# Hybrid decoder block on one core: the first modulation and the first norm made in another way

## The chip, the cores and the metric

The kernel runs on one core of a Trainium2 chip. The metric is the device time of one execution in microseconds (us): the median of three runs of the kernel before is 2028.79 (2028.37 to 2030.98). PE is TensorE (products), PEld its weight loads, DVE is VectorE, ACT is ScalarE, POOL is GpSimd, SP is SyncE, which here only issues loads.

## The reference

One sequence of 256 tokens with 2048 channels passes a decoder block. What matters here is its first step: a vector `c` gives a modulation, and the input's first norm is scaled and shifted by it before it meets the weights `w_in`.

```
c_act = silu(c)
mod = c_act @ w_ada + b_ada            # 2048 x 12288; sh1, sc1, g1, sh2, sc2, g2
h = rms_norm(x, norm1_g) * (1 + sc1) + sh1
x = x + g1 * hybrid_mixer(h, ...)      # h @ w_in, attention and SSD branches
h = rms_norm(x, norm2_g) * (1 + sc2) + sh2
x = x + g2 * swiglu(h, ...)
return rms_norm(x, final_g)
```

The norm divides each token by the root of the mean of its squares over the 2048 channels. `sh1` and `sc1` need the first 4096 columns of `w_ada`.

## The kernel before, in words

Everything is kept with channels on the 128 partitions and the 256 tokens along the free axis, so x is 16 tiles (`xs0`, `KT` = 16). Weights come from HBM in entries of one megabyte (128 x 2048), one load each, in a fixed list (`entries`); SP issues them (line 135) as buffers come free. Each weight entry is split by `Job.split`: ACT copies it to a rounded high part `wh` (line 181), DVE takes the difference as low part `wl` (line 182). Products are three matmuls per tile: high by high, high by low and low by high (lines 727 to 729).

The first products, with the first 5120 columns of `w_in` (`add_parts`), need h. Since h needs the modulation, and that needs 32 MB of `w_ada`, the 16 channel tiles are taken in five parts (`PARTS` = 2, 3, 4, 4, 3): once the modulation of a part's tiles is there, PE runs through all 40 output tiles with those tiles alone, and adds to partial sums. Sums of the first eight output tiles stay in PSUM (`res`); those of the others cycle through three banks (`cyc`) and are evacuated to SBUF (`part`) by ACT (line 696) or DVE.

The modulation of a part is made on DVE (`ada1_entries`): each row block of `w_ada` is multiplied by its element of `c_act` and added to an accumulator `aacc` (lines 403, 405), and at the end PE sums `aacc` over the partitions with single-column matmuls (`finish`, line 415: `aacc` is the weight, a column of ones the moving operand). DVE adds biases and gains (417 to 419), scales x (424), and ACT and DVE write h in a high and a low half (425, 426). The first part has four entries, loaded before everything else but x, which is loaded ahead of the fourth.

The first norm (`norm1`) is made once: ACT squares each of the 16 tiles (375), PE multiplies it by a matrix of ones and adds all up (376), so each partition has each token's sum; `inv_rms` takes the root on ACT (315) and the reciprocal on DVE (316), over 256 columns. Until x is there PE runs 14 products of ones (`warm`, line 383), whose result nothing uses.

The order of the instructions on each engine is fixed when the program is built; an engine works its list in that order, and each instruction waits for what it needs.

Of the kernel before, what the change touches and what calls it, by code (L numbers as in the profile page):

```python
# [9 lines left out]
F32 = mybir.dt.float32  # L10
F32R = mybir.dt.float32r
AF = mybir.ActivationFunctionType
ALU = mybir.AluOpType
# [3 lines left out]
P = 128  # L17
NACC = 4
NRES = 8
ZLEAD = 9  # L20
NWARM = 14
NCYC = 3
AHEAD = 2
BG = (4, 8, 8, 24, 4)
# [3 lines left out]
PARTS = (2, 3, 4, 4, 3)  # L28
NS = 40
L = 256  # L30
D = 2048
KT = D // P
# [3 lines left out]
LEAD1 = 2048 // (2048 // (256 * PARTS[0]) * 128)  # L36
# [11 lines left out]
def hybrid_block_kernel(  # L48
# [24 lines left out]
    act, dve, pool, pe = nc.scalar, nc.vector, nc.gpsimd, nc.tensor  # L73
# [12 lines left out]
    tmp = open_pool(ctx, "tmp", 2)  # L86
# [5 lines left out]
    cyc = [pcy.tile([P, 2, L], F32, name=f"cyc{i}") for i in range(NCYC)]  # L92
# [17 lines left out]
    def ps_side(name):  # L110
        return banks["side"].tile([P, 512], F32, tag="ps", name=name)
# [3 lines left out]
    state = {"loaded": 0, "done": 0}  # L115
# [68 lines left out]
    jobs = []  # L184
# [96 lines left out]
    ident = cst.tile([P, P], F32, name="ident")  # L281
    make_identity(nc, ident)
    ones = cst.tile([P, P], F32, name="ones")
# [17 lines left out]
    dve.tensor_scalar(cact, cc[:, C_C : C_C + 16], 0.5, None, op0=ALU.mult)  # L301
    dve.scalar_tensor_tensor(cact, ctmp, 1.0, cact, op0=ALU.add, op1=ALU.mult)
    dve.tensor_scalar(cc[:, C_CW : C_CB + 48], cc[:, C_CW : C_CB + 48], 0.5, None, op0=ALU.mult)

    d_z = dr.tile([32, P, L], F32, name="d_z")
    d_sa = dr.tile([16, P, L], F32, name="d_sa")
# [7 lines left out]
    def inv_rms(dst, ps, n):  # L314
        act.activation(dst, ps, AF.Sqrt, bias=eps[: dst.shape[0]], scale=1.0 / n)
        dve.reciprocal(dst, dst)
# [45 lines left out]
    p0 = open_pool(st0, "p0")  # L362
# [3 lines left out]
    def load_x():  # L366
        for q in range(4):
            nc.sync.dma_start(xs0[:, 4 * q : 4 * q + 4], x[4 * q : 4 * q + 4].rearrange("k p t -> p k t"))

    def norm1():  # L370

        ps = ps_side("n1")[:, :L]
        for k in range(KT):
            sq = tmp.tile([P, L], F32, tag="zv" if k % 2 else "zt", name="sq")
            act.activation(sq, xs0[:, k], AF.Square)
            pe.matmul(ps, ones, sq, start=(k == 0), stop=(k == KT - 1))
        inv_rms(xr, ps, D)

    def warm():

# [4 lines left out]
    def ada1_entries(k0, n):  # L385

        w = 256 * n
        per = 2048 // w
        off = 16 * P * 256 * k0
        res = []  # L390

        def fn_for(a, b):
            def fn(raw):
                if a == 0:
                    state["acc"] = p0.tile([P, 256 * max(PARTS)], F32, tag="aacc", name=f"aacc{k0}", bufs=2)
                acc = state["acc"][:, :w]
                hw = w // 2 if b == KT else w
                for c in range(0, w, hw):
                    for k in range(a, b):
                        o = w * (k - a) + c  # L400
                        r, v = raw[:, o : o + hw], acc[:, c : c + hw]
                        if k == 0:
                            dve.tensor_scalar(v, r, cact[:, 0:1], None, op0=ALU.mult)
                        else:
                            dve.scalar_tensor_tensor(v, r, cact[:, k : k + 1], v, op0=ALU.mult, op1=ALU.add)
                if b == KT:
                    with tc.high_priority(400):
                        finish(acc)

            return fn  # L410

        def finish(acc):
            ps = ps_side(f"ada{k0}")
            for b in range(2 * n):
                pe.matmul(ps[:, b : b + 1], acc[:, b * P : b * P + P], ones[:, 0:1], start=True, stop=True)
            sl = slice(k0, k0 + n)
            dve.tensor_tensor(s1[:, sl], ps[:, 0:n], cc[:, C_BADA + k0 : C_BADA + k0 + n], op=ALU.add)
            dve.tensor_tensor(a1[:, sl], ps[:, n : 2 * n], cc[:, C_BADA + 16 + k0 : C_BADA + 16 + k0 + n], op=ALU.add)
            dve.scalar_tensor_tensor(
                a1[:, sl], a1[:, sl], 1.0, cc[:, C_N1 + k0 : C_N1 + k0 + n], op0=ALU.add, op1=ALU.mult  # L420
            )
            for k in range(k0, k0 + n):
                x_, a_, s_ = xs0[:, k], a1[:, k : k + 1], s1[:, k : k + 1]
                dve.scalar_tensor_tensor(x_, x_, a_, xr, op0=ALU.mult, op1=ALU.mult)
                act.activation(h[:, k, :L], x_, AF.Identity, bias=s_)
                dve.scalar_tensor_tensor(h[:, k, L:], x_, s_, h[:, k, :L].bitcast(F32), op0=ALU.add, op1=ALU.subtract)
            if k0 + n == KT:
                st0.close()
                open_a1()

        for a in range(0, KT, per):
            b = min(a + per, KT)
            src = ada1[off + P * w * a : off + P * w * b].rearrange("(p f) -> p f", p=P)
            res.append((src, fn_for(a, b)))
        return res
# [273 lines left out]
    def add_parts():  # L709

        flat, k0 = [], 0
        starts, adas = [], []
        for r, n in enumerate(PARTS):
            starts.append(len(flat))
            adas.append(ada1_entries(k0, n))
            flat += [(r, m, k, k - k0, n) for m in range(NS) for k in range(k0, k0 + n)]
            k0 += n
        starts.append(len(flat))

        def body(tiles):  # L720
            def fn(wh, wl):
                for t, (r, m, k, c, n) in enumerate(tiles):
                    bank = res[m // 2] if m < NRES else cyc_at(r * NPAIR + (m - NRES) // 2)[2]
                    acc = bank[:, m % 2]

                    first = c == 0 and m % 2 == 0 and (r == 0 if m < NRES else r not in SEEDED)
                    pe.matmul(acc, wh[:, t], h[:, k, :L], start=first, stop=False, skip_group_check=True)  # L727
                    pe.matmul(acc, wh[:, t], h[:, k, L:], start=False, stop=False, skip_group_check=True)  # L728
                    pe.matmul(acc, wl[:, t], h[:, k, :L], start=False, stop=(c == n - 1), skip_group_check=True)  # L729
                    if c == n - 1 and m % 2:  # L730
                        part_done(r, m - 1)

            return fn

        entries.extend(adas[0])
        for g in range(len(flat) // 16):
            jobs.append(Job(w_s[g], body(flat[16 * g : 16 * g + 16])))
            for r in range(NP_ - 1):
                a, b = (max(0, (starts[i] - 16) // 16) for i in (r, r + 1))
                if a <= g < b:  # L740
                    q = adas[r + 1]
                    entries.extend(q[len(q) * (g - a) // (b - a) : len(q) * (g - a + 1) // (b - a)])
        state["nx"] = len(entries)
        state["nl"] = jobs[starts[NP_ - 1] // 16 - 1].entry
# [532 lines left out]
    hook(jobs[NS + 2], lambda: (flush(), gens.append(index_gen())))  # L1277
    hook(jobs[first_pair], open_a2)
    warm()
    load_to(LEAD1 - 1)  # L1280
    load_x()
    load_to(LEAD1)
    norm1()
    run_jobs()
    flush()
    drain()
# [119 lines left out]
```

## Time and profile before

| | |
|---|---|
| median of 3 runs | 2028.79 us |
| the profiled execution | 2029.8 us |
| its span | 2028.1 us |
| DVE busy | 1460.4 us (72%) |
| ACT busy | 1057.4 us (52%) |
| mean DMA rate over the span | 243 GB/s |

The span runs from the first to the last instruction of the program; the execution's own time has some 1.7 us around it. A matmul of f32 operands shows up as two passes in the trace; so the 14 warm-up products are 28 rows. Two passes overlap, so a group's mean is longer than the distance from one to the next. The granted clock is a share of 2.4 GHz: 0.50 is 1.2 GHz.

### The profile page before, as it was taken

Reading aid. Unit: us, or ns where it says so; the run is one execution under the profiler, and the core shown is the slowest. Engines: PE = TensorE matmul, PEld = TensorE weight load, DVE = VectorE, ACT = ScalarE, POOL = GpSimd, SP = SyncE. Lnnn points to the kernel's source line nnn. Section 1 sums busy time; section 2 is a strip of 40 time slices with the busy share of each in tenths; the row PEclk is TensorE's granted clock in tenths of the full one; section 3 lists DMA queues with packets and bytes.
Section 4 is the critical chain, followed back from the end, with each engine's and each line's share of the span. In section 5 each row is a group of like instructions: output and inputs, shape, how many; then the busy total and the mean of one; then the engine's idle time right before and its main releaser. Section 6 shows DMA issues by size and latency. Waiting matters only on the chain.

```text
span 2028.1 us, 31920 instructions
## 1 busy us (share of the span) xinstructions
PE 1988.5 (98%) x12964; PEld 1791.2 (88%) x12964; DVE 1460.4 (72%) x1832; ACT 1057.4 (52%) x1427; POOL 159.5 (8%) x161
## 2 busy tenths in 40 slices
PE   8999999999999999999999999999999999999997
PEld 6899998899888888898989988888888888888887
DVE  6777787977678898888888865668786555544443
ACT  4655475565345766677654444554444444443442
POOL 0000000220000111101113211000000000000000
PEclk8999999999999999999999999999999999999999
DMA  9888767666887767666676876467776555565552
GB/s 376 333 304 303 271 230 276 223 243 235 296 325 257 254 230 261 245 230 246 220 263 231 284 263 218 163 227 274 282 275 218 192 192 187 192 224 189 193 183 100
DMA packets 102339, 492.30 MB, mean 243 GB/s; under 512 B 10768, under 2 KB 45952, under 8 KB 48688
## 3 DMA queue, kind: packets, MB, share of 16 engines
q1 hardware_dynamic: 100528, 486.19, 66.8%
q0 software_dynamic: 704, 3.15, 0.4%
q8 instruction: 102, 1.67, 0.3%
q10 hardware_dynamic: 960, 0.92, 0.1%
q14 instruction: 45, 0.37, 0.1%
HBM read 475.44 MB, written 17.92 MB: 243 GB/s over the span
## 4 chain that ended last, share of the span: by engine, by line
PE 77%; issue 8%; DVE 7%; DMA 4%; ACT 3%; POOL 0%; SPq 0%; DVEq 0%; ACTq 0%; POOLq 0%
PE acc_gu L250 15%; PE acc_gu L252 8%; PE acc_dn L250 7%; PE acc_cv L250 6%; PE acc_dn L252 4%; PE acc_cv L252 4%; DVE wl L182 3%; PE acc_z L250 3%; PE acc_out L250 2%; PE acc_pb L210 2%; PE cyc L729 2%; PE cyc L727 2%; PE acc_pb L211 2%; PE acc_pb L212 2%; PE cyc L728 2%
## 5 line engine op out<-in xcount | busy, mean ns | idle before, releaser
L182 DVE TENSOR_TENSOR wl<-raw,wh 128x2048 fp32r<-128x2048 f32 (+1 forms) x316 | 722.1, 2286 | 319.0 <-ACT wh L181 311.5
L181 ACT ACTIVATE wh<-raw 128x2048 fp32r<-128x2048 f32 (+1 forms) x316 | 599.2, 1897 | 390.8 <-PE acc_dn L250 95.1
L250 PE MATMUL acc_gu<-h,wh 128*128 128x512 f32 x1312 | 313.1, 391 | 0.0
L250 PEld LDWEIGHTS acc_gu<-h,wh 128*128 128x128 f32 x1312 | 241.1, 188 | 46.7
L250 PE MATMUL acc_cv<-h,wh 128*128 128x512 f32 x768 | 193.7, 402 | 0.0
L252 PEld LDWEIGHTS acc_gu<-h,wl 128*128 128x128 f32 x1312 | 168.2, 191 | 6.4
L449 DVE SCALAR_TENSOR_TENSOR acc<-raw,cact,acc 128x1024 f32<-128x1024 f32 x120 | 156.7, 1306 | 23.4 <-DMA raw<-in_ada_dram 22.9
L250 PEld LDWEIGHTS acc_cv<-h,wh 128*128 128x128 f32 x768 | 142.2, 191 | 32.7 <-issue 4.6
L252 PE MATMUL acc_gu<-h,wl 128*128 128x256 f32 x1312 | 170.2, 283 | 0.0
L250 PE MATMUL acc_dn<-ffact,wh 128*128 128x512 f32 x660 | 160.0, 392 | 0.0
L727 PE MATMUL cyc<-h,wh 128*128 128x256 f32 x512 | 148.0, 290 | 5.1 <-ACT cyc L702 1.8
L729 PE MATMUL cyc<-h,wl 128*128 128x256 f32 x512 | 144.9, 288 | 2.9 <-DVE wl L182 2.9
L728 PE MATMUL cyc<-h,wh 128*128 128x256 f32 x512 | 146.3, 286 | 0.0
L210 PE MATMUL acc_pb<-y,wh 128*128 128x256 f32 x512 | 145.6, 284 | 0.0
L211 PE MATMUL acc_pb<-y,wh 128*128 128x256 f32 x512 | 143.1, 279 | 0.0
L212 PE MATMUL acc_pb<-y,wl 128*128 128x256 f32 x512 | 142.8, 279 | 0.0
L250 PEld LDWEIGHTS acc_dn<-ffact,wh 128*128 128x128 f32 x660 | 120.2, 188 | 23.1
L250 PE MATMUL acc_z<-h,wh 128*128 128x512 f32 x512 | 123.1, 393 | 0.0
L250 PEld LDWEIGHTS acc_z<-h,wh 128*128 128x128 f32 x512 | 93.9, 188 | 20.6 <-issue 2.3
L727 PEld LDWEIGHTS cyc<-h,wh 128*128 128x128 f32 x512 | 99.9, 195 | 7.8 <-ACT cyc L702 3.0
L252 PEld LDWEIGHTS acc_cv<-h,wl 128*128 128x128 f32 x768 | 99.0, 191 | 5.0 <-issue 1.2
L252 PE MATMUL acc_cv<-h,wl 128*128 128x256 f32 x768 | 102.4, 284 | 0.0
(331 smaller groups left out, 3357.7 us busy)
## 6 DMA issues: line engine op xcount, KB each, us to landing
raw<-in_w_gu_dram SPq DMA_DIRECT2D x88, 1024.0 KB, 4.7
raw<-in_ada_dram SPq DMA_DIRECT2D x75, 1024.0 KB, 5.1
raw<-in_w_ssm_dram SPq DMA_DIRECT2D x48, 1024.0 KB, 5.2
raw<-in_w_dn_dram SPq DMA_DIRECT2D x44, 1024.0 KB, 4.7
raw<-in_w_z_dram SPq DMA_DIRECT2D x32, 1024.0 KB, 5.1
raw<-in_w_pb_dram SPq DMA_DIRECT2D x32, 1024.0 KB, 5.1
raw<-in_w_s_dram SPq DMA_DIRECT2D x27, 1024.0 KB, 6.3
raw<-in_w_pa_dram SPq DMA_DIRECT2D x16, 1024.0 KB, 5.9
```

The source lines that it names most:

```text
L181: act.activation(whf[:, o], raw[:, o], AF.Copy)
L182: dve.tensor_tensor(wlf[:, o], raw[:, o], whf[:, o].bitcast(F32), op=ALU.subtract)
L210: pe.matmul(acc, wh, rhs[:, :L], start=first, stop=False)
L211: pe.matmul(acc, wh, rhs[:, L:], start=False, stop=False)
L212: pe.matmul(acc, wl, rhs[:, :L], start=False, stop=last)
L250: pe.matmul(acc, wh[:, t], rhs(k), start=n == 0, stop=False, skip_group_check=True)
L252: pe.matmul(acc[:, :L], wl[:, t], rhs(k)[:, :L], start=False, stop=n == end, skip_group_check=True)
L449: dve.scalar_tensor_tensor(a, r, cact[:, k : k + 1], a, op0=ALU.mult, op1=ALU.add)
L727: pe.matmul(acc, wh[:, t], h[:, k, :L], start=first, stop=False, skip_group_check=True)
L728: pe.matmul(acc, wh[:, t], h[:, k, L:], start=False, stop=False, skip_group_check=True)
L729: pe.matmul(acc, wl[:, t], h[:, k, :L], start=False, stop=(c == n - 1), skip_group_check=True)
```

## The change

The first part's modulation is no longer accumulated on DVE. As each of its four entries lands, PE takes every 128 x 128 block of it as weight and the column `cact[:, k]` as moving operand, and adds over the 16 row blocks in PSUM: 64 matmuls of one column (new line 418). The other four parts stay as they were. The squares of x are taken two tiles at a time on ACT and added by DVE to one tile of 512 columns; PE sums that over the partitions into two columns of 128 tokens (new line 386), root and reciprocal are taken of these two columns, and two matmuls with the identity spread the result over all partitions into a PSUM bank (394), from which DVE scales x; a copy goes to `xr` for the later parts. The table for the root is loaded near the start (304). x is loaded after all four entries, the warm-up has 6 products in place of 14, `aacc` has one buffer in place of two, and the first weight entry is split in four pieces of 512 columns. `finish` is cut into `finish`, `modulation` and `scale`.

```
-NWARM = 14
+NWARM = 6
...
+    act.activation(ctmp[:, 0:1], eps, AF.Sqrt)
...
+    def squares():
+        for k in range(0, KT, 2):
+            sq = p0.tile([P, 2, L], F32, tag="sq", name="sq", bufs=2) if k else state["sum"]
+            act.activation(sq, xs0[:, k : k + 2], AF.Square)
+            if k:
+                dve.tensor_tensor(state["sum"], state["sum"], sq, op=ALU.add)
...
     def norm1():
-        ps = ps_side("n1")[:, :L]
-        for k in range(KT):
-            sq = tmp.tile([P, L], F32, tag="zv" if k % 2 else "zt", name="sq")
-            act.activation(sq, xs0[:, k], AF.Square)
-            pe.matmul(ps, ones, sq, start=(k == 0), stop=(k == KT - 1))
-        inv_rms(xr, ps, D)
+        ps = cyc[1][:, 0]
+        for i in range(2):
+            for c in range(2):
+                pe.matmul(
+                    ps[:, c : c + 1], state["sum"][:, i, c * P : c * P + P], ones[:, 0:1],
...
+        r = tmp.tile([P, 2], F32, tag="rcol", name="rcol")
+        inv_rms(r, ps[:, 0:2], D)
+        n1["r"] = cyc[2][:, 0]
+        for c in range(2):
+            pe.matmul(n1["r"][:, c * P : c * P + P], r[:, c : c + 1].to_broadcast([P, P]), ident, start=True, stop=True)
...
             def fn(raw):
+                if k0 == 0:
+                    if a == 0:
+                        state["ps"] = ps_side("ada0")
+                    for k in range(a, b):
+                        for i in range(2 * n):
+                            o = w * (k - a) + i * P
+                            pe.matmul(
+                                state["ps"][:, i : i + 1], raw[:, o : o + P], cact[:, k : k + 1],
...
+                    if b == KT:
+                        with tc.high_priority(400):
+                            squares()
+                            norm1()
+                            for v in (s1, a1):
+                                dve.tensor_copy(v[:, 0:2], state["sum"][:, :, 0])
+                            modulation(state["ps"])
+                            scale(n1["r"])
+                            act.activation(xr, n1["r"], AF.Copy)
+                    return
...
-            jobs.append(Job(w_s[g], body(flat[16 * g : 16 * g + 16])))
+            jobs.append(Job(w_s[g], body(flat[16 * g : 16 * g + 16]), piece=512 if g == 0 else 2048))
...
     warm()
-    load_to(LEAD1 - 1)
+    load_to(LEAD1)
     load_x()
-    load_to(LEAD1)
-    norm1()
+    state["sum"] = p0.tile([P, 2, L], F32, name="sum")
     run_jobs()
```

What the change does to the lists. PE at the start of the program, before (`cyc` is the warm-up's bank, `n` the norm's sums, `ada` the modulation, `res` the first products):

```order
L383 MATMUL cyc_70<-ones 128x512 x14
L376 MATMUL n_174<-sq,ones 128x256 x16
L415 MATMUL ada_254<-ones,aacc_231 128x1 x4
L727 MATMUL res_76<-h,wh_270 128x256
L727 MATMUL res_77<-h,wh_270 128x256
```

And PE at the same place in the changed kernel (`part` is where the entries of `w_ada` land, `sum` the sum of squares, `rcol` the root's two columns):

```order
L400 MATMUL cyc_70<-ones 128x512 x6
L418 MATMUL ada_174<-cact,part 128x1 x64
L386 MATMUL cyc_71<-ones,sum 128x1 x4
L394 MATMUL cyc_72<-ident,rcol 128x128 x2
L772 MATMUL res_76<-h,wh_286 128x256
```

The 64 single-column matmuls now stand ahead of the norm's, and both ahead of the first product.

DVE from the first accumulation on, before (`aacc_231` is the first part's accumulator, `aacc_275` the second part's):

```order
L403 TENSOR_SCALAR aacc_231<-part,cact 128x512
L405 SCALAR_TENSOR_TENSOR aacc_231<-part,cact,aacc_231 128x512 x11
L405 SCALAR_TENSOR_TENSOR aacc_231<-part,cact,aacc_231 128x256 x5
L316 RECIPROCAL xr<-xr 128x256
L405 SCALAR_TENSOR_TENSOR aacc_231<-part,cact,aacc_231 128x256 x3
L182 TENSOR_TENSOR wl_271<-part,wh_270 128x2048
L417 TENSOR_TENSOR s_110<-ada_254,cc 128x2
L418 TENSOR_TENSOR a_109<-ada_254,cc 128x2
L403 TENSOR_SCALAR aacc_275<-rawy,cact 128x768
L419 SCALAR_TENSOR_TENSOR a_109<-a_109,cc 128x2
L405 SCALAR_TENSOR_TENSOR aacc_275<-rawy,cact,aacc_275 128x768
L424 SCALAR_TENSOR_TENSOR xs_148<-xs_148,a_109,xr 128x256 x2
```

DVE at the same place in the changed kernel (the second part's accumulator is now `aacc_297`):

```order
L379 TENSOR_TENSOR sum<-sum,sq 128x512 x7
L428 COPY s_110<-sum 128x2
L428 COPY a_109<-sum 128x2
L460 TENSOR_TENSOR s_110<-ada_174,cc 128x2
L461 TENSOR_TENSOR a_109<-ada_174,cc 128x2
L317 RECIPROCAL rcol<-rcol 128x2
L462 SCALAR_TENSOR_TENSOR a_109<-a_109,cc 128x2
L469 SCALAR_TENSOR_TENSOR xs_149<-xs_149,a_109,cyc_72 128x256 x2
L182 TENSOR_TENSOR wl_287<-part,wh_286 128x512
L471 SCALAR_TENSOR_TENSOR h<-xs_149,s_110,h 128x256 x2
L182 TENSOR_TENSOR wl_287<-part,wh_286 128x512 x3
L442 TENSOR_SCALAR aacc_297<-rawy,cact 128x768
```

The accumulations of the second part now stand behind the first part's modulation, h and the whole first split; before, three of them stood ahead of h.

ACT from the first weight split on, before (`wh_270`, `wh_283`, `wh_297` are the first three weight entries, `part<-cyc` evacuations of a bank):

```order
L181 ACTIVATE wh_270<-part 128x2048
L425 ACTIVATE h<-xs_148,s_110 128x256 x2
L181 ACTIVATE wh_283<-raw_229 128x2048
L181 ACTIVATE wh_297<-part 128x2048
L696 ACTIVATE part<-cyc_70 128x512
L696 ACTIVATE part<-cyc_71 128x512
L696 ACTIVATE part<-cyc_72 128x512
```

ACT in the changed kernel (`wh_286`, `wh_305`, `wh_319` are the same three entries):

```order
L181 ACTIVATE wh_286<-part 128x512 x2
L470 ACTIVATE h<-xs_149,s_110 128x256 x2
L431 ACTIVATE xr<-cyc_72 128x256
L181 ACTIVATE wh_286<-part 128x512 x2
L181 ACTIVATE wh_305<-raw_172 128x2048
L741 ACTIVATE part<-cyc_70 128x512
L741 ACTIVATE part<-cyc_71 128x512
L741 ACTIVATE part<-cyc_72 128x512
L181 ACTIVATE wh_319<-part 128x2048
```

The third entry's split has moved behind three evacuations. From the fourth entry's split on, all engines' lists are the same as before.

## Rows read from the trace of the kernel before

**Rows 1.** The page's first part: busy time, share of the span, instructions.

```profile
PE 1988.5 (98%) x12964; PEld 1791.2 (88%) x12964; DVE 1460.4 (72%) x1832; ACT 1057.4 (52%) x1427; POOL 159.5 (8%) x161
```

**Rows 2.** Timeline of PE, 0 to 36 us: start, duration, what, [idle before, releaser].

```profile
1.21 14.12 PE L383 MATMUL cyc<-ones 128*128 128x512 f32 x28 [1.21 <-POOL ones L284]
15.16 7.07 PE L376 MATMUL n<-sq,ones 128*128 128x256 f32 x32
26.32 1.84 PE L415 MATMUL ada<-ones,aacc 128*128 128x1 f32 x8 [4.08 <-DVE aacc L405]
32.00 1.22 PE L727 MATMUL res<-h,wh 128*128 128x256 f32 x4 [3.84 <-ACT h L425]
```

**Rows 3.** Chain of waits up to 32 us: start, duration, what.

```profile
22.32 1.28 ACT L315
...
24.12 1.75 DVE xr L316
...
27.00 2.28 DVE wl L182
...
30.92 0.49 DVE xs L424
```

**Rows 4.** Stretches: length, busy time of each engine, PEclk (granted clock), DMA share, GB/s.

```profile
22.30:25.40 3.10, 0.00 (x0) 0.00 (x0) 1.28 (x1) 3.07 (x3) 0.00 (x0) 1.00 1.03 426
25.40:28.80 3.40, 1.84 (x8) 1.78 (x8) 3.36 (x5) 0.48 (x1) 0.00 (x0) 0.50 0.99 417
29.34:62.98 33.64, 28.09 (x210) 26.95 (x210) 27.82 (x36) 16.47 (x21) 0.00 (x0) 0.91 0.94 369
36.00:48.00 12.00, 12.00 (x102) 12.00 (x101) 10.82 (x10) 3.94 (x6) 0.00 (x0) 1.00 0.95 362
63.00:108.20 45.20, 43.73 (x341) 42.57 (x341) 34.31 (x27) 27.18 (x35) 0.00 (x0) 0.96 0.85 326
803.70:807.10 3.40, 3.40 (x33) 3.40 (x31) 1.78 (x4) 3.03 (x4) 0.00 (x0) 1.00 0.96 352
807.10:810.50 3.40, 3.40 (x10) 2.72 (x11) 3.04 (x6) 3.36 (x5) 0.00 (x0) 0.50 0.24 96
```

**Rows 5.** Timeline of PE, 804.8 to 807.3 us, single-column matmuls.

```profile
805.01 0.50 PE L323 MATMUL yn<-ones,ysqa 128*128 128x1 f32 x4
805.37 2.01 PE L453 MATMUL ada<-ones,acc 128*128 128x1 f32 x16
```

**Rows 6.** Timeline of PE near 1276 us: a root spread by the identity.

```profile
1275.81 0.71 PE L335 MATMUL n2b<-ident,rcol 128*128 128x128 f32 x4 [0.84 <-DVE rcol L316]
```

**Rows 7.** Timeline of PEld in the warm-up: two neighbouring passes.

```profile
12.59 0.19 PEld L383 LDWEIGHTS cyc<-ones 128*128 128x128 f32 x1 [0.24 <-issue]
13.02 0.19 PEld L383 LDWEIGHTS cyc<-ones 128*128 128x128 f32 x1 [0.24 <-issue]
```

**Rows 8.** Timeline of DVE, 20 to 63 us.

```profile
20.10 2.07 DVE L405 SCALAR_TENSOR_TENSOR aacc<-part,cact,aacc 128x256 f32<-128x256 f32 x5 [4.32 <-DMA part<-in_ada_dram]
...
29.34 0.61 DVE L403 TENSOR_SCALAR aacc<-rawy,cact 128x768 f32<-128x768 f32 x1
...
36.57 4.17 DVE L405 SCALAR_TENSOR_TENSOR aacc<-raw,cact,aacc 128x768 f32<-128x768 f32 x4
...
50.91 2.29 DVE L182 TENSOR_TENSOR wl<-raw,wh 128x2048 fp32r<-128x2048 f32 x1 [3.87 <-ACT wh L181]
...
59.03 0.16 DVE L417 TENSOR_TENSOR s<-ada,cc 128x3 f32<-128x3 f32 x1 [1.60 <-PE ada L415]
...
60.69 2.29 DVE L182 TENSOR_TENSOR wl<-part,wh 128x2048 fp32r<-128x2048 f32 x1
```

**Rows 9.** Timeline of ACT near 48 us: an evacuation and a weight split.

```profile
48.48 0.60 ACT L696 ACTIVATE part<-cyc 128x512 f32<-128x512 f32 x1 [0.84 <-PE cyc L729]
48.97 1.90 ACT L181 ACTIVATE wh<-raw 128x2048 fp32r<-128x2048 f32 x1
```

**Rows 10.** Timeline of SP: issue of a load.

```profile
29.32 0.33 SPq L135 DMA_DIRECT2D part<-in_w_s_dram  x1
```

More of the change, by code (lines that the diff above doesn't have):

```diff
@@ L368, in load_x @@
             nc.sync.dma_start(xs0[:, 4 * q : 4 * q + 4], x[4 * q : 4 * q + 4].rearrange("k p t -> p k t"))
-    def norm1():
-        ps = ps_side("n1")[:, :L]
-        for k in range(KT):
-            sq = tmp.tile([P, L], F32, tag="zv" if k % 2 else "zt", name="sq")
-            act.activation(sq, xs0[:, k], AF.Square)
-            pe.matmul(ps, ones, sq, start=(k == 0), stop=(k == KT - 1))
-        inv_rms(xr, ps, D)
+    n1 = {}
+    def squares():
[4 more added lines that the diff above has]
+                dve.tensor_tensor(state["sum"], state["sum"], sq, op=ALU.add)
+    def norm1():
+        ps = cyc[1][:, 0]
[3 more added lines that the diff above has]
+                    ps[:, c : c + 1], state["sum"][:, i, c * P : c * P + P], ones[:, 0:1],
+                    start=(i == 0 and c == 0), stop=(i == 1), skip_group_check=True,
+                )
+        r = tmp.tile([P, 2], F32, tag="rcol", name="rcol")
[3 more added lines that the diff above has]
+            pe.matmul(n1["r"][:, c * P : c * P + P], r[:, c : c + 1].to_broadcast([P, P]), ident, start=True, stop=True)
     def warm():
@@ L393, in fn @@
             def fn(raw):
+                if k0 == 0:
[6 more added lines that the diff above has]
+                                state["ps"][:, i : i + 1], raw[:, o : o + P], cact[:, k : k + 1],
+                                start=(k == 0 and i == 0), stop=(k == KT - 1), skip_group_check=True,
+                            )
+                    if b == KT:
[8 more added lines that the diff above has]
+                    return
                 if a == 0:
-                    state["acc"] = p0.tile([P, 256 * max(PARTS)], F32, tag="aacc", name=f"aacc{k0}", bufs=2)
+                    state["acc"] = p0.tile([P, 256 * max(PARTS)], F32, tag="aacc", name=f"aacc{k0}", bufs=1)
                 acc = state["acc"][:, :w]
@@ L408, in fn @@
                         finish(acc)
+                        scale(xr)
             return fn
@@ L415, in finish, with modulation @@
                 pe.matmul(ps[:, b : b + 1], acc[:, b * P : b * P + P], ones[:, 0:1], start=True, stop=True)
+            modulation(ps)
+        def modulation(ps):
             sl = slice(k0, k0 + n)
@@ L421, in finish, with scale @@
             )
+        def scale(xr):
             for k in range(k0, k0 + n):
```

## The prediction

> **What bounds the kernel now.** I read the engine shares first. PE is busy 98% of the span [rows 1], so time can only be won or lost where PE stands still or runs at its lower clock, and the change touches one such place, the first 70 us. PE's own timeline comes next [rows 2]: a block of warm-up products, then the sums of the first norm, a hole in which only the small `ada` sums run, and at 32.00 the first product with real weights. The reader is to see that everything before 32.00 is a lead-in. The chain of waits says what made it that long [rows 3]: when the norm's sums end, a table load of 1.28, a root, a reciprocal of 256 columns (1.75), a weight split on DVE (2.28), which stands ahead of the modulation, then from 30.92 the scaling and the split of h, 1.08 up to the product. The granted clock by stretch [rows 4] shows that PE stood still from 22.3 and was at 0.50 (1.2 GHz) from 25.4 on. Last come the timelines of DVE and ACT from 29 to 63 [rows 8, 9]: DVE multiplies up the next part's modulation, is busy 27.82 of 33.64 [rows 4], and stands still once for 3.87 (behind ACT) and once for 1.60 (behind PE).
>
> **The stream of single columns.** New on PE: 64 matmuls of one column, two passes each, as the four `ada` matmuls of line 415 show up as eight passes [rows 2]. So 128 passes, each with a weight load of 128 columns. What precedes them: six warm-up matmuls are twelve passes in place of 28. The sums began at 15.16 [rows 2] and a pass takes 0.43 at the full clock (12.59 to 13.02) [rows 7], so sixteen fewer begin the stream at 15.16 - 16 x 0.43 = 8.3. Before it ends all that was loaded ahead of it is there (the last piece had landed at 20.10 [rows 8], and the same six megabytes are ordered, x now last).
>
> What does a pass cost? At 26.32 eight take 1.84 with a mean of 351 ns, so (1.84 - 0.35) / 7 = 0.213 apart, at a clock of 0.50 [rows 2, 4]. At 805.37 sixteen take 2.01, so (2.01 - 0.25) / 15 = 0.117 apart, at 1.00 [rows 4, 5]. The stream lasts 15.0 by the one and 27.3 by the other; which one holds decides the case.
>
> Rows 4 and 5 answer it, I think. From 805.01 to 807.1 PE ran nothing but passes of one column, back to back; PE and its weight loads are both busy 3.40 of 3.40 in that stretch, and yet the clock in the next is 0.50. So such passes did not hold the clock, though nothing stood still. In the stretch after the norm it fell some 3.1 after the last wide product (22.3 to 25.4). I let it fall 3.1 after the stream begins: 3.1 / 0.117 = 26 passes, the other 102 x 0.213 = 21.7, end at 8.3 + 3.1 + 21.7 = 33.1. Falling after 2.1 instead gives 33.8; never at the full clock 35.6; never falling 23.3.
>
> The Trainium skill speaks against this: by "TensorE: Matmul & The Clock Gate", section "What's actually happening", the clock follows how busy PE has been, and by its section "Why this matters for your kernels" it is idle gaps between bursts that throw it back; a stream without gaps would then keep 2.4 GHz. The rows at 803.7 to 810.5 say otherwise for this kind of pass. The same page's section "LDWEIGHTS (loading the stationary operand)" gives columns / 1.2, 107 ns for 128 columns, whatever the clock, and by it the stream would end at about 22; the measured 0.213 at the lower clock decides.
>
> **From the stream to the first product.** The first norm's squares are no longer summed by PE but by DVE: eight squares of 512 columns on ACT, seven adds on DVE. No row shows these sizes here; four times as wide, a split takes 1.90 on ACT and 2.29 on DVE [rows 8, 9], so the two squares and two adds that can still be due after 20.1 end before 28.5. Covered by the stream; without that cover they would cost at most 8.4, and a quarter of it (some 2) is nearer. The table load moves ahead of x, the reciprocal shrinks from 256 columns to two: both leave the path. What stays, behind the stream: eight passes of column sums as in line 415's row, 1.84, to 34.9; root, reciprocal and hand-overs 0.84 (rcol's hole ahead of line 335) [rows 6], to 35.8; four passes that spread the root, 0.71 at the full clock [rows 6], some 1.0 at the lower one (3 x 0.213 + 0.38), to 36.8; scaling and split of h as before, 1.08, to 37.9. That DVE reads the factor from PSUM is shown by no row; I keep the 0.49 of [rows 3] for a piece; twice that would add 0.5, half would take 0.2 away. First product at 37.9 against 32.00: **+5.9**.
>
> **Behind the first product.** DVE stands in its order behind the stream, since the modulation waits for PE and all of the next part's accumulations are queued behind it. In the kernel before they began at 29.34 [rows 8], now after xs, four quarter splits and h: 36.8 + 0.9 + 4 x 0.6 + 0.9 = 41.0. From there to the end of the split at 60.69 + 2.29 = 62.98 [rows 8] DVE had 27.82 of work [rows 4], less the 1.7 for the first part's xs and h, plus 1.60 waiting for PE's sums: 27.7. So at the earliest 41.0 + 27.7 = 68.7, **+5.7**. That uses up the 3.87 of standing still. Does it come back? On ACT the split for the third weight block now stands behind three evacuations. The second block's low half is done, after four accumulations (0.61 and three of 4.17 / 4 [rows 8]) and its own split, at 41.0 + 3.7 + 2.29 = 47.0; the order has 30 products from there to the third evacuation, at 0.118 (102 in 12.00 [rows 4]) 3.5; evacuation and split are 0.60 and 1.90 [rows 9]: 53.0. DVE is through with the accumulations between (4.17 [rows 8]) at 51.2, so stands still 1.8. The next block repeats this behind three more evacuations: 53.0 + 2.3 + 20 x 0.118 + 2.5 = 60.2 against 55.3 + 4.2 = 59.5, 0.7. Together 2.5: the part's end at 71.2 instead of 62.98, **+8.2**. PE, which waited for that split, resumes as much later.
>
> From 63 to 108.2 PE is busy 43.73 of 45.20 [rows 4], and the order of all engines is unchanged from there: nothing takes the delay back. The reduction of `aacc` to one buffer and the split of the first block in quarters cost nothing beyond what is counted; the quarter split lets PE start 1.7 earlier than a whole one would, which is in the sum. The profiled execution took 2029.8 (span 2028.1), 1.0 above the median of 2028.79; the difference is added to the median: 2028.8 + 8.2 = **2037.0**.
>
> **Rivals.** *The clock holds.* Then the stream ends at 23.3, sums 1.1, 0.84, 0.71 and 1.08 follow, first product at 27.0, 5.0 earlier. DVE begins the next part at 30.1, and its 27.7 of work ends at 57.8, or at 60.3 with the same 2.5 of standing still: 2.7 to 5.2 gained, 2023.6 to 2026.1, at the middle 2024.9. For it: PE never stands still in the stream, and sixteen single-column passes at 805.37 did run at the full clock throughout. Against it: the 0.50 right behind them. It decides from the first 10 us of the stream. It is what the rule of the Trainium skill cited above would do here. *The delay is partly given back.* The ACT holes don't open, since ACT's splits could find their evacuations done; then +5.7, 2034.5; and if the hole of PE near 60 swallows two more, 2032. For it: the 2.5 rests on a product count and on hand-overs that no row shows. Against it: DVE alone reaches 68.7. *The loads run dry.* SP's next load of weights was issued at 29.32 [rows 10], when the first split released its buffer; now that is at 41.0, and the queue has nothing more to issue in between. The loads ran at 0.94 of the DMA time from 29 to 63 [rows 4]. If the third block and what follows come late, another 2 to 4: 2041. Against it: nothing else contends for the first of them.
>
> **How the numbers follow.** Chances: the sum as it stands (2035 to 2039.5) 0.51; partly given back (2030.5 to 2035) 0.24; the clock holds 0.15; loads late (above 2039.5) 0.10. What a measurement here can tell from no change is 0.2%, 4.1 us: 2024.7 to 2032.9. Faster needs the clock to hold and no standing still on DVE: about half of that case, 0.07. Within: the other half and a quarter of the second case, 0.14. Slower 0.79. The range leaves out the clock's case and the two thin ends: 2030.5 to 2041.
>
> **What would show it.** Right: rows of `ada0` about 0.21 apart from some 12 us on, granted clock 0.50 until well after the first product, that product between 36.5 and 39, DVE idle from about 22 to 33 behind PE, the split that ended at 62.98 ending near 71. Wrong in the first step: `ada0` at 0.12 apart and done by 24. Wrong in the second: first product near 38 but that split ending below 68. Wrong in the last: the lead of the kernel before at 63 us found smaller at 120 us. If a pass of one column costs less than 0.21 at the lower clock in a long stream than in eight, all terms shrink.

## The result and the profile after

The changed kernel takes 2041.83 us (median of 4 runs, 2039.68 to 2044.06), the kernel before 2028.58 beside it (4 runs, 2025.11 to 2030.98): a ratio of 1.0055, with a 95% interval of 1.0036 to 1.0074. It is slower, by 13.2 us as the difference of the medians and by 11.2 by the ratio, which need not be that of the medians; the prediction had 8.2. By the ratio the time is 2028.79 x 1.0055 = 2039.9, inside the stated range; the median lies 0.8 above its upper end of 2041. The profiled execution took 2044.06, with a span of 2042.3 against 2028.1, so 14.2 more in the traces.

The timeline of PE in the lead-in, after (start, duration, what, [idle before, releaser]):

```profile
1.21 7.86 PE L400 MATMUL cyc<-ones 128*128 128x512 f32 x12 [1.21 <-POOL ones L284]
8.90 23.58 PE L418 MATMUL ada<-cact,part 128*128 128x1 f32 x128
32.34 1.84 PE L386 MATMUL cyc<-ones,sum 128*128 128x1 f32 x8
34.83 1.19 PE L394 MATMUL cyc<-ident,rcol 128*128 128x128 f32 x4 [0.64 <-DVE a L462]
37.14 0.79 PE L772 MATMUL res<-h,wh 128*128 128x256 f32 x2 [1.11 <-ACT h L470]
```

Against [rows 2], one block of 128 passes stands where the norm's products and the hole stood, and the first product comes at 37.14 and not at 32.00. The stretches of the same time, after (length, busy time of PE, PEld, DVE, ACT, POOL, granted clock, DMA share, GB/s):

```profile
9.00:13.00 4.00, 4.00 (x39) 4.00 (x37) 0.00 (x0) 0.00 (x0) 0.00 (x0) 1.00 0.99 417
13.00:16.40 3.40, 3.40 (x18) 3.40 (x18) 0.00 (x0) 0.86 (x2) 0.00 (x0) 0.50 1.07 354
16.40:32.30 15.90, 15.90 (x76) 15.90 (x76) 5.08 (x9) 3.95 (x7) 0.00 (x0) 0.50 0.97 386
32.30:43.70 11.40, 9.59 (x42) 8.95 (x43) 7.98 (x16) 5.31 (x9) 0.00 (x0) 0.50 0.22 76
```

Read the granted clock beside PE's busy time. PE and its weight loads are busy without a gap from 9.00 to 32.30, and from 13.00 on the clock is 1.2 GHz all the same; a pass then takes 15.90 / 76 = 0.209 us. It comes back only at 43.7, among the products.

DVE up to the split that ended at 62.98 before, after:

```profile
32.52 0.16 DVE L460 TENSOR_TENSOR s<-ada,cc 128x2 f32<-128x2 f32 x1 [9.87 <-PE ada L418]
40.05 0.61 DVE L442 TENSOR_SCALAR aacc<-rawy,cact 128x768 f32<-128x768 f32 x1
53.05 2.29 DVE L182 TENSOR_TENSOR wl<-part,wh 128x2048 fp32r<-128x2048 f32 x1 [2.93 <-ACT wh L181]
60.52 2.29 DVE L182 TENSOR_TENSOR wl<-raw,wh 128x2048 fp32r<-128x2048 f32 x1 [1.09 <-ACT wh L181]
68.64 0.16 DVE L460 TENSOR_TENSOR s<-ada,cc 128x3 f32<-128x3 f32 x1 [1.60 <-PE ada L455]
70.30 2.29 DVE L182 TENSOR_TENSOR wl<-part,wh 128x2048 fp32r<-128x2048 f32 x1
179.56 0.16 DVE L460 TENSOR_TENSOR s<-ada,cc 128x4 f32<-128x4 f32 x1 [2.03 <-PE ada L455]
```

And ACT where it holds DVE up, after:

```profile
50.62 0.60 ACT L741 ACTIVATE part<-cyc 128x512 f32<-128x512 f32 x1 [0.60 <-PE cyc L774]
51.11 1.90 ACT L181 ACTIVATE wh<-part 128x2048 fp32r<-128x2048 f32 x1
```

DVE stands still 9.87 behind the stream, begins the second part's accumulations at 40.05 (29.34 in [rows 8]), and stands still twice more, 2.93 and 1.09, behind a split that ACT runs after its third evacuation. That part's end moves from 62.98 to 70.30 + 2.29 = 72.59. In [rows 8] 12.07 us lie between the start of DVE's fourth split (50.91) and the end of the fifth (62.98), and here just as many, from 60.52 to 72.59.

From here on a "lag" is the start of an instruction less the start of the same one in the trace of before. The modulation of the fourth part, the last row of DVE's above, is a good mark, since from 63 us on both kernels do the same work. Before it stands at 171.22 in DVE's timeline:

```profile
171.22 0.16 DVE L417 TENSOR_TENSOR s<-ada,cc 128x4 f32<-128x4 f32 x1 [2.03 <-PE ada L415]
```

So the lag there is 179.56 - 171.22 = 8.34, and it stays between 7.6 and 9.2 until 510 us. That is near the predicted 8.2. It is less than the 72.59 - 62.98 = 9.61 at the part's end, and the granted clock shows where the difference can come from. The stretch of 45.2 us behind that end, after:

```profile
72.60:117.80 45.20, 43.24 (x346) 41.83 (x346) 34.49 (x29) 28.11 (x37) 0.00 (x0) 1.00 0.90 343
```

The same stretch of before has 0.96 in [rows 4]: there PE ran at 1.2 GHz once more, from 62.98 for 3.4 us, and here it did not. Half of 3.4 is 1.7, an estimate of what that costs, beside the 1.3 that came back. But the traces end 14.2 apart: another 5 to 6 us are lost later, where the prediction saw nothing.

PE's waits late in the program, first of before, then of after:

```profile
645.14 2.23 PE L453 MATMUL ada<-ones,acc 128*128 128x1 f32 x16 [2.19 <-DVE acc L449]
751.23 0.68 PE L335 MATMUL ynb<-ident,rcol 128*128 128x128 f32 x4 [0.69 <-DVE rcol L316]
```

```profile
655.21 3.57 PE L498 MATMUL ada<-ones,acc 128*128 128x1 f32 x16 [3.65 <-DVE acc L494]
764.61 0.68 PE L336 MATMUL ynb<-ident,rcol 128*128 128x128 f32 x4 [2.63 <-DVE rcol L317]
```

The stretches around the first of these waits, of before and then of after:

```profile
646.65:650.07 3.42, 3.42 (x11) 2.84 (x12) 2.66 (x5) 0.42 (x1) 0.00 (x0) 0.50 1.01 410
650.07:653.49 3.42, 3.42 (x22) 3.01 (x21) 1.92 (x3) 1.00 (x1) 0.00 (x0) 1.00 0.46 115
```

```profile
654.70:658.10 3.40, 2.89 (x14) 2.89 (x14) 1.33 (x3) 0.42 (x1) 0.00 (x0) 0.50 0.88 340
658.10:661.50 3.40, 3.40 (x11) 2.82 (x11) 2.68 (x5) 0.42 (x1) 0.00 (x0) 0.50 0.64 263
```

The first wait is 1.46 longer and the second 1.94, and the lower clock holds for 6.8 us and not for 3.4, which costs half of 3.4, an estimate. Together 1.46 + 1.94 + 1.7 = 5.1 of what came on top. Behind the second wait stands a load; DVE, after, and that load as issued at 743.94 (size, us from issue to landing):

```profile
751.71 1.28 DVE L494 SCALAR_TENSOR_TENSOR acc<-raw,cact,acc 128x1024 f32<-128x1024 f32 x1 [2.33 <-DMA raw<-in_ada_dram]
raw<-in_ada_dram SPq DMA_DIRECT2D x1, 1024.0 KB, 7.8
```

In the kernel before the same load took 5.1.

### The profile page after: what moved, and what is told of

It is laid out like the page before. It is cut to its first block, busy times and chain, and to the rows that moved or that the text cites. A ratio compares the mean times of both kernels' runs of the same rounds, so it can differ in the third digit from the quotient of the medians.

```text
span 2042.3 us, 32074 instructions
## 1 busy us (share of the span) xinstructions
PE 2003.1 (98%) x13048; PEld 1809.6 (89%) x13048; DVE 1450.2 (71%) x1824; ACT 1056.1 (52%) x1424; POOL 162.1 (8%) x161
## 4 chain that ended last, share of the span: by engine, by line
PE 86%; DVE 6%; ACT 2%; DMA 2%; issue 1%; POOL 1%; SPq 0%; DVEq 0%; ACTq 0%; POOLq 0%
PE acc_gu L250 15%; PE acc_gu L252 8%; PE acc_dn L250 7%; PE acc_cv L250 6%; PE acc_z L250 5%; PE acc_dn L252 4%; PE acc_cv L252 3%; DVE wl L182 3%; PE cyc L774 3%; PE cyc L772 3%; PE acc_out L250 3%; PE cyc L773 3%; PE acc_pb L210 2%; PE acc_pb L211 2%; PE acc_z L252 2%; PE acc_pb L212 2%
## 5 line engine op out<-in xcount | busy, mean ns | idle before, releaser
L774 PEld LDWEIGHTS cyc<-h,wl 128*128 128x128 f32 x512 | 98.5, 195 | 5.4 <-DVE wl L182 5.3
```

## The experiments

Nothing is left out of the computation in any of them. The lags at 171 us come from the mark above. The later ones are taken over all of DVE's instructions, paired by order, as the median of nine neighbours. "Part's end" is the lag of the end of DVE's split that stood at 62.98 before, and "low clock" the time at 1.2 GHz between 60 and 76 us, which is 3.4 in the kernel before. A kernel is compared with runs of the kernel before on the same chip (medians 2030.65, 2029.58 and 2029.32); "over before" is the difference of medians. The ratios need not be those of the medians: that of "512 columns moving" gives 2.8 us and not 0.3.

| | over before | part's end | low clock | lag at 171 | at 800 | at 1250 us |
|---|---|---|---|---|---|---|
| the changed kernel | 13.2 | 9.6 | 0 | 8.3 | 14.0 | 14.1 |
| again | 12.6 | 9.6 | 0 | 8.3 | 13.6 | 14.2 |
| before, first product late | 6.0 | 1.8 | 0 | 0.6 | 6.1 | 8.4 |
| norm alone | 9.3 | 3.8 | 6.8 | 5.4 | 5.8 | 9.7 |
| 512 columns moving | 0.3 | 1.5 | 0 | 0.1 | -4.2 | 3.1 |
| DVE's work ahead | 7.5 | 4.4 | 0 | 3.0 | 0.0 | -0.4 |
| ACT's split ahead | 10.8 | 6.7 | 0 | 5.8 | 8.8 | 11.1 |
| 512 columns, DVE ahead | 0.6 | 3.0 | 0 | 1.5 | -2.6 | -1.2 |
| before, late shift | 12.5 | 0.9 | 3.4 | 1.0 (9.0 at 250) | 11.4 | 17.6 |
| 512 columns, ACT ahead | -2.7 | -1.3 | 6.8 | 0.4 | -0.3 | 1.1 |

The profiled execution is one of the runs. That of "DVE's work ahead" was the fastest of its twelve (2029.47, median 2037.09), that of "late shift" the slowest of its six, so the columns behind 171 us are to be read with care. Compare "part's end" with "lag at 171": the lag falls by 0.9 to 1.5 in the kernels without low clock there, stays with 3.4 us of it, and grows by 1.6 and 1.7 with 6.8. So part of the lag at 171 goes with the clock in those few us.

**The changed kernel again**, with no edit.

> The changed kernel once more, unchanged. Theory A (the loss is made in the first 72 us and only carried on; what came on top of it between 577 and 800 us was chance of that execution): the lag against the kernel before is 8 to 9 at 120 us and the time 8 to 10 above it. Theory B (a late start costs again in the stretch where loads are short, 500 to 800 us): lag 8 to 9 at 120 us, but 12 to 14 at 820 us and in the time, as in the first measurement.

2043.26 against 2030.65, ratio 1.0064 (1.0050 to 1.0077). The mark is at 179.49, the two late waits are 3.29 and 2.83: the early loss and the late one both come back, as theory B had it.

**The kernel before with a late first product:**

```
-NWARM = 14
+NWARM = 24
```

> The kernel before with 24 warm-up products in place of 14: nothing but a later start. Ten more products are 20 passes of 0.43, so the first real product comes at 32.0 + 8.6 = 40.6 in both theories, with the clock at 2.4 GHz until the norm is done. Theory A: the lag stays as it is, time 8 to 9 above the kernel before. Theory B: the lag grows to 12 to 14 by 820 us. If the first 30 us have slack that I did not see, the time is less than 6 above.

PE, then DVE, of this kernel:

```profile
40.08 1.22 PE L727 MATMUL res<-h,wh 128*128 128x256 f32 x4 [5.01 <-ACT h L425]
```

```profile
29.85 0.61 DVE L403 TENSOR_SCALAR aacc<-rawy,cact 128x768 f32<-128x768 f32 x1
171.84 0.16 DVE L417 TENSOR_TENSOR s<-ada,cc 128x4 f32<-128x4 f32 x1 [2.03 <-PE ada L415]
```

The first product is 8.1 late, three us more than in the changed kernel, and at 171 us 0.6 of it is left. Both theories had it carried on; the third case, slack that was not seen, is the nearest. DVE's accumulations begin 0.5 later than they did, since the order that was fixed for this kernel puts four of them ahead of the norm's reciprocal. What is left at the part's end, 1.8, is that reciprocal (1.75), now behind the start of the accumulations, less 1.0 by which DVE's hole behind ACT is shorter (2.86 and not 3.87), and small pieces. So a late first product costs little, 1.8 by the part's end, as long as DVE's work does not wait with it. The kernel still ends 6.0 above before (ratio 1.0028, 1.0013 to 1.0043), in its trace all lost behind 500 us.

**The new norm without the stream:** the first part's modulation is summed by DVE as before, the rest of the change stays, with 14 warm-up products.

```
-NWARM = 6
+NWARM = 14
...
-                if k0 == 0:
-                    if a == 0:
-                        state["ps"] = ps_side("ada0")
...
                 if b == KT:
                     with tc.high_priority(400):
+                        if k0 == 0:
+                            squares()
+                            norm1()
                         finish(acc)
...
```

> The single-column stream is undone: the first part is accumulated on DVE as before, 14 warm-up products; all else of the change stays (squares added by DVE, two-column root, early table, x loaded last, quarter splits, ACT's split of the third block behind three evacuations). Theory (the stream at 1.2 GHz is the loss): DVE ends its accumulations near 19, the squares' sum comes near 23.4, first product at 29 to 30; the second part's accumulations begin near 32.5, the split that ended at 62.98 ends at 62.5 to 64, time 0 to 1.5 above the kernel before and 11 to 13 below the changed one. Rival (the norm's new way or the new order on DVE and ACT is the loss): first product after 34, time over 5 above the kernel before.

PE, then DVE:

```profile
30.49 0.79 PE L755 MATMUL res<-h,wh 128*128 128x256 f32 x2 [1.11 <-ACT h L453]
```

```profile
33.40 0.61 DVE L420 TENSOR_SCALAR aacc<-rawy,cact 128x768 f32<-128x768 f32 x1
176.57 0.16 DVE L443 TENSOR_TENSOR s<-ada,cc 128x4 f32<-128x4 f32 x1 [2.03 <-PE ada L438]
```

A miss. The first product is 1.5 earlier than before, and yet the lag is 5.4 (2039.98, ratio 1.0044, 1.0028 to 1.0060). Its accumulations begin 4.06 later, since DVE now runs xs, h and the quarter splits ahead of them; before, they stood between. The part ends 3.8 late, and the rest of the 5.4 comes behind it, where PE runs at the lower clock for 6.8 us and not for 3.4. So late accumulations cost even when the first product is early; but ACT's new order is in this run too, and how much of the 3.8 is its own the run does not tell.

**The stream with the operands exchanged:** cact's column is the weight and 512 columns of ada's block move; 32 passes, and the row is turned back by four small products.

```
...
-    state["ps"][:, i : i + 1], raw[:, o : o + P], cact[:, k : k + 1],
-    start=(k == 0 and i == 0), stop=(k == KT - 1), skip_group_check=True,
+    state["ps"][0:1, :w], cact[:, k : k + 1], raw[:, w * (k - a) : w * (k - a) + w],
+    start=(k == 0), stop=(k == KT - 1),
...
```

> The changed kernel with the operands of the stream exchanged: the column of c_act is the weight, a row block of 512 columns moves, so 16 matmuls of 512 columns (32 passes) make one row, which DVE copies and four small matmuls turn into columns. Theory (the clock falls because a single moving column is no work to the gate): the clock stays at 1.00, passes 0.43 apart, the stream takes 13.8 and ends near 22.5, first product at 26 to 28, the split that ended at 62.98 ends at 59.5 to 61.5, time 1.5 to 4 below the kernel before. Rival (a single active weight column does not hold the clock either): passes 0.85 apart from about 12 on, stream end near 34, time as the changed kernel.

The stretches of its stream (columns as above), then DVE:

```profile
8.90:12.90 4.00, 4.00 (x10) 0.76 (x9) 0.00 (x0) 0.00 (x0) 0.00 (x0) 1.00 1.01 425
12.90:16.40 3.50, 3.50 (x10) 0.69 (x9) 0.00 (x0) 0.96 (x2) 0.00 (x0) 1.00 1.05 348
16.40:22.10 5.70, 5.70 (x14) 0.99 (x12) 3.46 (x5) 3.85 (x7) 0.00 (x0) 1.00 1.07 390
```

```profile
31.32 0.61 DVE L450 TENSOR_SCALAR aacc<-rawy,cact 128x768 f32<-128x768 f32 x1
171.33 0.16 DVE L468 TENSOR_TENSOR s<-ada,cc 128x4 f32<-128x4 f32 x1 [2.03 <-PE ada L463]
```

PE is as busy as in the changed kernel, from the same place, and keeps 2.4 GHz. The stream ends at 22.1 and not at 32.3, the accumulations begin at 31.32, the lag is 0.1 (2030.97, ratio 1.0014, 0.9999 to 1.0029). The 1.5 to 4 below before that were expected did not come. So the loss hangs on the kind of pass, not on giving these sums to PE. The exchange changes the moving columns, the weight loads and the number of passes at once; which of them the clock goes by is not shown.

**DVE's work ahead of the modulation.** A product of nothing (the accumulator's first column times 0.0, added to the sum of squares) makes the first norm follow DVE's first four accumulations; the scheduler then put the quarter splits ahead too, and the third block's split on ACT ahead of the evacuations.

```
+first = state["sum"][:, 0, 0:1]
+dve.scalar_tensor_tensor(first, state["acc"][:, 0:1], 0.0, first, op0=ALU.mult, op1=ALU.add)
...
```

> The changed kernel with DVE's first four accumulations of the second part (3.7 us) and the four quarter splits of the first weight block (2.4) put ahead of the first part's modulation, and the third block's split on ACT ahead of the evacuations; the stream of single columns and the first norm stay. Theory A (what costs is DVE's work that is queued behind the stream): the accumulations begin near 24 to 26 us and not at 40.05; the first product stays near 37 to 38; the lag against the kernel before at 120 to 400 us falls from 8.3 to between 1 and 4, and the time to about 2030 to 2037. Theory B (the late first product itself costs): the lag stays above 6, the time above 2038.

PE, then DVE:

```profile
37.06 1.23 PE L781 MATMUL res<-h,wh 128*128 128x256 f32 x4 [1.11 <-ACT h L479]
```

```profile
26.83 0.62 DVE L448 TENSOR_SCALAR aacc<-rawy,cact 128x768 f32<-128x768 f32 x1
55.36 2.29 DVE L182 TENSOR_TENSOR wl<-raw,wh 128x2048 fp32r<-128x2048 f32 x1 [5.13 <-ACT wh L181]
174.25 0.17 DVE L469 TENSOR_TENSOR s<-ada,cc 128x4 f32<-128x4 f32 x1 [2.03 <-PE ada L464]
```

The stream and the first product stay where they were, the accumulations begin at 26.83, and the lag falls from 8.3 to 3.0, within the 1 to 4 that were expected. ACT's order is moved here as well, which by the next run is worth 2.5 by itself, so 2.8 is left for DVE's if the two add up. The 3.0 that remains goes with the late products: DVE waits 5.13 for a split that ACT runs behind their evacuations. 2037.09, ratio 1.0035 (1.0021 to 1.0048).

**ACT's split ahead**, in the changed kernel: three writes of one element make the first three evacuations follow the third block's split.

```
+if r == 0 and m < NRES + 6:
+    act.activation(v[:, 0, 0:1], jobs[2].wh[:, 0, 0:1].bitcast(F32), AF.Copy)
```

> The changed kernel with the third weight block's split on ACT put ahead of the first three evacuations and nothing else moved. If DVE's two idle stretches behind that order (2.93 at 53.05 and 1.09 at 60.52) are a cost of their own, as the prediction had it: both all but gone, the lag at 120 to 400 us falls from 8.3 to between 4.5 and 6, the time to about 2038. Rival: the split would have waited for its load or for a buffer anyway; the idle stretches stay in another place, the lag at 8.

ACT, then DVE:

```profile
44.93 1.92 ACT L181 ACTIVATE wh<-part 128x2048 fp32r<-128x2048 f32 x1 [4.42 <-DMA part<-in_w_s_dram]
```

```profile
57.67 2.29 DVE L182 TENSOR_TENSOR wl<-raw,wh 128x2048 fp32r<-128x2048 f32 x1 [1.33 <-ACT wh L181]
177.01 0.16 DVE L460 TENSOR_TENSOR s<-ada,cc 128x4 f32<-128x4 f32 x1 [2.03 <-PE ada L455]
```

The split now waits for its load and is done at 46.85, before DVE asks for it: the 2.93 is gone, the other stays at 1.33, and the lag falls by 2.5 to 5.8. The ACT order is a cost of its own. 2040.34, ratio 1.0043 (1.0030 to 1.0056), two us more than expected.

**The kernel before, once more** (one execution, no edit).

> The kernel before, unchanged, looked at once more. The stretches from 540 to 800 and from 1100 to 1200 us, where weights arrive just in time, added some 5 us to the loss of the changed kernel, twice, and between -4 and +8 in the other runs. If that is chance in the loads: the second look differs from the first by 2 us or more in one of these stretches and by under 0.5 before 500 us. If it follows from the change: the second look keeps within 1 us of the first everywhere.

2028.74. Its lag against the first trace is 0.7 at 171 us, 0.1 at 800 and -0.7 at 1250. That is neither case as written: above 0.5 ahead of 500 us, and less than 2 us of difference in the late stretches. So one more trace does not show that chance makes the late loss; the runs of before beside it lie between 2025.76 and 2037.06.

**Both: 512 columns moving, and DVE's work ahead.**

> The two that help together: the sums of the first part's modulation made with cact's column as the weight and 512 columns moving (clock held), and DVE's accumulations and quarter splits ahead of the modulation. If DVE's work from 29 to 63 us is what bounds that stretch, DVE starts some 6 us earlier than before, and the lag at 120 to 400 us is between -3 and -6, the time about 2023 to 2027. Rival: the loads (0.94 of the DMA time from 29 to 63) bound it as soon as DVE is ahead: the lag is between 0 and -1.5, the time within 2 us of before.

PE, then DVE:

```profile
31.17 1.86 PE L388 MATMUL cyc<-ones,sum 128*128 128x1 f32 x8 [6.64 <-DVE sum L384]
```

```profile
27.15 0.61 DVE L456 TENSOR_SCALAR aacc<-rawy,cact 128x768 f32<-128x768 f32 x1
53.98 2.29 DVE L182 TENSOR_TENSOR wl<-raw,wh 128x2048 fp32r<-128x2048 f32 x1 [4.82 <-ACT wh L181]
```

A miss: 2030.15, ratio 1.0002 (0.9988 to 1.0015), lag 1.5. Tying the norm to the accumulations made PE stand still for 6.64 ahead of the norm's sums and put the first product off to 35.98, so DVE's head start was lost behind ACT, which evacuates what PE makes. Neither theory had that. The reading that fits is that this end is set by the later of two chains, DVE's from its accumulations and PE's from its first product.

**The kernel before, shifted late:** one product is issued 68 times where the fourth part begins.

```
-pe.matmul(acc, wh[:, t], h[:, k, :L], start=first, stop=False, skip_group_check=True)
+for _ in range(68 if first and r == 3 and m == NRES else 1):
+    pe.matmul(acc, wh[:, t], h[:, k, :L], start=first, stop=False, skip_group_check=True)
```

> The kernel before with one product of 256 columns issued 68 times over (the same result each time) where the fourth part begins, behind 171 us: PE is busy 67 x 0.118 = 7.9 us longer there, and all that comes later is 7.9 late, while the first 170 us are as before. Theory A (the extra 5 us that the changed kernel lost between 540 and 1190 us follow from the lag itself, whatever made it): lag 7.9 at 250 to 400 us, 11 to 13 from 800 us on, time near 2041 to 2043. Theory B (they follow from something else in the change, or the stage takes whatever lag comes): lag 7 to 9 throughout, time near 2037.5.

PE's two late waits, and the stretches around the first:

```profile
655.02 3.58 PE L453 MATMUL ada<-ones,acc 128*128 128x1 f32 x16 [2.38 <-DVE acc L449]
762.62 0.68 PE L335 MATMUL ynb<-ident,rcol 128*128 128x128 f32 x4 [0.70 <-DVE rcol L316]
```

```profile
654.80:658.20 3.40, 3.18 (x15) 3.18 (x16) 1.04 (x3) 0.42 (x1) 0.00 (x0) 0.50 0.92 369
658.20:661.60 3.40, 3.40 (x10) 2.72 (x11) 2.97 (x5) 0.42 (x1) 0.00 (x0) 0.50 0.53 214
```

Theory A by the time and by the lag at 800 us. The lead-in is that of before, the shift makes a lag of 9.0 from 250 us on (1.0 of it was there already), and it grows to 11.4 by 660 us, as in the changed kernel, with the same 6.8 us at the lower clock. 2041.87 against 2029.32, ratio 1.0052 (1.0039 to 1.0066): 12.5 for a delay of 8. In this trace a lag that reaches 500 us grows without anything else of the change; the time alone does not show it, since its interval, 7.9 to 13.4 us, just holds 8 too. And the second late wait is that of before, 0.70 and not 2.63. The load behind it was issued at 743.88, with the lag that it has in the changed kernel, and landed sooner:

```profile
raw<-in_ada_dram SPq DMA_DIRECT2D x1, 1024.0 KB, 5.0
```

So that part of the late loss does not follow from the lag. The lag of 17.6 at 1250 us grew at yet another place, in the slowest of six executions.

**512 columns moving, ACT's split ahead**, DVE's order left alone (the edits of the fourth and the sixth experiment).

> The kernel with 512 moving columns in the stream, and the third weight block's split on ACT ahead of the evacuations (DVE's accumulations left where they were, behind the modulation). With the stream at full clock it had a lag of 0.1 at 120 to 400 us and DVE stood still behind ACT for 2.28 and 2.40. If ACT's order sets these: the first is gone, the lag goes to -1.5 to -2.5 and the time to about 2027 to 2029, under both kernels. Rival: PE's products, not ACT's order, set the later of the two; lag within 0.7 of before, time within 2 us of it.

DVE of this kernel:

```profile
32.02 0.61 DVE L450 TENSOR_SCALAR aacc<-rawy,cact 128x768 f32<-128x768 f32 x1
49.70 2.29 DVE L182 TENSOR_TENSOR wl<-raw,wh 128x2048 fp32r<-128x2048 f32 x1 [1.33 <-ACT wh L181]
171.66 0.17 DVE L468 TENSOR_TENSOR s<-ada,cc 128x4 f32<-128x4 f32 x1 [2.04 <-PE ada L463]
```

2026.59 (12 runs, 2021.42 to 2031.93), ratio 0.9986 (0.9975 to 0.9998): faster than both kernels, by 2.7 us against the kernel before, near the 2027 to 2029 that were expected. The profiled execution (2031.14) is one of its slower ones and shows a lag of 0.4, not the -1.5 to -2.5 that were expected. At the part's end it is 1.3 ahead of before; then PE runs at the lower clock from 60.86 to 67.69, twice as long as before, and the lead is gone. Whether the faster executions keep it is not shown.

## Why the prediction was right, and where not

- **The clock falls in the stream: right.** At 13.0, so 4.1 behind the first pass and not 3.1. With the pass at 0.209 and not 0.213 the stream ends at 32.3 (33.1 forecast). With the operands exchanged the same sums did not bring it down, so it was this kind of pass. By the rule of the Trainium skill weighed in the prediction ("TensorE: Matmul & The Clock Gate", section "What's actually happening") a busy PE would have kept its clock. Here PE was busy in both streams (3.40 of 3.40 and 15.90 of 15.90 us in one, 5.70 of 5.70 in the other) and kept it in one; the measurement decides.
- **From the stream to the first product: right in size.** 37.14 - 32.3 = 4.8, as forecast (37.9 - 33.1). The squares, the adds, the table load and the factor in PSUM were hidden or cheap, as put. But its +5.9, printed in bold as if a term, is none by itself: eight us of it, with DVE's accumulations begun only 0.5 later than before, cost 1.8 by the part's end.
- **Behind the first product: right in mechanism, and this is the step that decides.** With the orders of DVE and ACT put back ahead, 5.3 of the lag of 8.3 is gone. Accumulations at 40.05 (41.0), ACT's third split done at 53.01 (53.0), DVE's split of the block after it begun at 60.52 (60.2). The sum then added the two holes to DVE's floor of 27.7 and came to 71.2. With the 12.07 that [rows 8] give from that split's start to the part's end, counted from ACT's own 60.2, the end would have been 72.3; measured 72.59. The term was 1.4 too small: the holes came to 2.93 + 1.09 = 4.0 and not 2.5 and DVE's work to 0.8 more than its floor, while it began 1.0 earlier.
- **"Nothing takes the delay back": wrong twice.** Of the 9.6 at the part's end 1.3 came back before 171 us, beside a clock that stayed up where it fell before; that 8.2 is so well met there is luck. And behind 500 us some 5 more were lost. This is the step that failed: the prediction held that a delay is carried through unchanged where the order is the same. With the same order PE waited longer behind DVE and one load, and ran longer at the lower clock: 1.46 + 1.94 + 1.7 = 5.1. In the kernel before, with nothing but a shift of 8, the lag also grew, to 11.4 by 660 us, but not at the second wait.
- **The rival "loads run dry"** gave 2041 from another place. SP's load was indeed issued at 40.16 and not at 29.32, and the queue stood idle from 33.4 until then, but the block landed at 44.90, before ACT came to it at 51.11. That rival's number fits by accident; what it named did not happen at 30 to 60 us. The stated range went up to 2041 for its sake, so that a time near 2040 lies inside it is partly luck too.

What stays open is why the late stage adds. In the traces it is longer waits of PE and more time at the lower clock. Between 500 and 1260 us PE's waits (those above 0.3) and its time at 1.2 GHz sum to 6.5 and 6.8 us in the kernel before, 9.2 and 10.2 in the changed one, 12.8 and 13.7 with the late first product, and 4.0 and 0 with DVE's work ahead, whose trace wins 3.4 us between 171 and 1250 us. But the kernel with a lag of 0.6 at 171 us lost more, 7.8 by 1250 us, than the changed kernel with 8.3, which lost 5.8, and the two with 512 columns moving and lags of 0.1 and 1.5 ended at 0.3 and 0.6 above before by their medians. So it is not a function of the lag alone, and no run told what else it hangs on.

## What to carry to other kernels

Price a longer lead-in by the engine that has the work queued behind it, and not only by when the first product starts: here a product 8 us late cost 1.8 by the part's end while DVE's work ran on, and putting DVE's and ACT's work ahead took 5.3 of 8.3 away with the product as late as it was. The rest needs the product too: the later of the two chains sets the end. Where a delay opens a hole on the waiting engine, follow the chain of the engine it waits for to the end, and do not add the hole to a floor. A few us of lower clock behind the changed place can give back or add as much as a small term of the sum, so read the granted clock there before a lag is put down to the change. And where a stage lives from weights that land just in time, a delay that reaches it need not come out the same size.

## What the runs showed of the hardware

- Two streams of matmuls that keep PE busy throughout end at different clocks: with one moving column and 128 weight columns the granted clock fell from 2.4 to 1.2 GHz after 4.1 us, with 512 moving columns and one weight column it stayed at 2.4 for all of 13.9 us, with PEld busy 2.44 of 13.20 against 15.90 of 15.90.
- The first part's weights go through PE in 32 passes and 13.89 us as moving columns, and in 128 passes and 23.58 us as weights, most of them at the lower clock.
- A pass of one column with a weight load of 128 columns took 0.117 us at the granted clock 1.00 (sixteen at 805.37, before) and 0.209 at 0.50 (the stream, after).
- The same load of one megabyte, issued at 743.94 and at 743.88 us in two kernels, took 7.8 and 5.0 us to land.
